# A transformer layer on one core: longer warm-up, angle tables written later, and one column block of the last layer norm on TensorE and ScalarE

## The chip, the cores and the metric

The kernel runs on one core of one Trainium2 chip. The metric is the device time of one execution in microseconds; the kernel before has a median of 1452.82 us over three runs.

## The reference, cut to what matters

One decoder layer for 256 tokens of width 2048, in float32. The projection feeds a retention branch and a sliding-window attention branch; their gated sum goes through an output projection, a layer norm, a SwiGLU feed-forward block and a second layer norm.

```python
proj = h @ w_in
ret = retention_branch(rq, rk, rv, rg, ...)              # rotary angles from positions
att = sliding_window_sink_attention(aq, ak, av, sinks, positions)
merged = sigmoid(gate_a) * ret + sigmoid(gate_b) * att
h = layer_norm(ALPHA * h + merged @ w_out, ln1_g, ln1_b)
ffn = (silu(h @ w_gate) * (h @ w_up)) @ w_down
h = layer_norm(ALPHA * h + ffn, ln2_g, ln2_b)            # (z - mean) * rsqrt(var + eps) * g + b
```

## The kernel before, in words

Every large product is a stream of *chunks*. A chunk gives 512 output columns for both halves of the tokens (t = 0 and t = 1, 128 tokens each). Its weights come in blocks by the queue of SyncE (`raw`), ScalarE rounds them (`wh`, line 192), VectorE makes the rest (`wl`, line 193), and TensorE adds three matmuls for each 128 rows of the weight and each t: `wh` by `xh` (line 208), `wl` by `xh` (209), `wh` by `xl` (210). So line 209 can't begin before the whole `wl` of its block is there. The first chunk is special: its weights come together with the columns of x in nine blocks (`xraw`), and x itself is split into `xh` and `xl` (lines 422 and 423) on the way. It is followed by four chunks of attention queries, four for retention's queries and keys, and the rest.

Beside the stream, small jobs (Python generators) are stepped twice after each step of the stream by `pump`; what they write is interleaved with the stream. The tile framework then schedules: it sets each engine's final order by its own model of what is ready, so the order in which the code is written is not the order in which an engine gets its instructions. Names in the code and in the rows:

- `tables` (from line 428): sine and cosine of the rotary angles; some 35 VectorE instructions on 128x272 values, then three sines on ScalarE.
- `akv_bg` (504): rotates the attention keys and transposes them to `kT`; `attention` (524): one job for each key head g and each t. It makes its scores (line 543) in two banks of the pool `mx`. The eight query heads of a group lie in pairs over the upper and lower 64 partitions (u = 0, 1); a score matmul uses 64 rows of TensorE, those of u = 0 write one bank, those of u = 1 the other. VectorE reads them from the bank (line 546).
- `NWARM` matmuls on zeros (403) run before the first data is there.
- `ln2` (740): for the last layer norm, mean and variance, then for each of four column blocks two VectorE instructions (lines 728 and 729) and a DMA of the result.

Of the kernel before, what the change touches and what calls it, by code (L numbers as in the profile page):

```python
# [9 lines left out]
F32 = mybir.dt.float32  # L10
F32R = mybir.dt.float32r
I32 = mybir.dt.int32
AF = mybir.ActivationFunctionType
ALU = mybir.AluOpType
RIGHT = "right"

P = 128
SEQ = 256
DM = 2048
DFF = 5632  # L20
C = 512
# [3 lines left out]
HD = 64  # L25
NSPL = 3
NSPL0 = 3
NWARM = 2
AKD = 7
NQ = 3  # L30
NGEN = 3
PC = 2
# [23 lines left out]
NFR = 136  # L56
LINE = 32
NFL = 144
# [37 lines left out]
def layer_kernel(ctx, tc, a, out):  # L96
    nc = tc.nc
# [12 lines left out]
    def bank(kind, shape):  # L110
        if "all" in psp:
            return psp["all"].tile(shape, F32, name="bank")
        return psp[kind].tile(shape, F32, name=kind)
# [25 lines left out]
    def drain():  # L139
        while bg:  # L140
            pump(1)
# [215 lines left out]
    jobs = {}  # L357
# [3 lines left out]
    ident = cst[:, 0:P]  # L361
# [4 lines left out]
    def bcast_cols(dram, c0, n):  # L366
        return dram[0:1, c0:c0 + n].broadcast_to([P, n])
# [33 lines left out]
    for i in range(NWARM):  # L401
        wp = bank("tr", [P, C])
        nc.tensor.matmul(wp, lhsT=warm[:, 0:P], rhs=warm[:, P:P + C], start=True, stop=True)

    XS = [1, 1, 2, 2, 2, 2, 2, 2, 2]
    xraw = {}

    def x_dma(b):
        k = sum(XS[:b])
        r = ini.tile([P, max(XS), SEQ + C], F32, name="xraw", bufs=XB)  # L410
        nc.sync.dma_start(out=r[:, 0:XS[b]], in_=a["xw"][:, k:k + XS[b]])
        xraw[b] = r
        if b == 2:
            nc.scalar.dma_start(out=cst[:, 0:NC0], in_=a["consts"][:, 0:NC0])
            xraw["pos"] = ini.tile([P, LINE], I32, name="posi")[:, 0:2]
            nc.scalar.dma_start(out=xraw["pos"], in_=a["pos"])

    def x_cast(b):
# [7 lines left out]
        return xh[:, k, t * P:(t + 1) * P], xl[:, k, t * P:(t + 1) * P]  # L426

    def tables():
        posi = xraw["pos"]
        posf = ini.tile([P, 2], F32, name="posf")  # L430
        nc.vector.tensor_copy(out=posf, in_=posi)
        ang = ini.tile([P, 2, NFR], F32, name="ang")
        for t in range(2):
            nc.vector.tensor_scalar(out=ang[:, t], in0=freq, scalar1=posf[:, t:t + 1], scalar2=None, op0=ALU.mult)
        yield
        SH = [P, 2, NFR]
        cur = ang
        digs = []
        for i, e in enumerate((20, 8, -4)):
            m = 1.5 * 2.0 ** (23 + e)  # L440
            d = ini.tile(SH, F32, name=f"dig{i}")
            nc.vector.tensor_scalar(out=d, in0=cur, scalar1=m, scalar2=m, op0=ALU.add, op1=ALU.subtract)
            nc.vector.tensor_sub(out=cur, in0=cur, in1=d)
            digs.append(d)
            yield
        c20 = _digits(20, -12, -24)
        c8 = _digits(8, -12, -24)
        c4 = _digits(-4, -18, -30)
        M0 = 1.5 * 2.0 ** 23
        hi = None  # L450
        tmp = ini.tile(SH, F32, name="ttmp")
        for i, cc in enumerate((c20, c8, c4)):
            t = ini.tile(SH, F32, name=f"th{i}")
            nc.vector.tensor_scalar(out=t, in0=digs[i], scalar1=cc[0], scalar2=None, op0=ALU.mult)
            nc.vector.tensor_scalar(out=tmp, in0=t, scalar1=M0, scalar2=M0, op0=ALU.add, op1=ALU.subtract)
            nc.vector.tensor_sub(out=t, in0=t, in1=tmp)
            if hi is None:
                hi = t
            else:
                nc.vector.tensor_add(out=hi, in0=hi, in1=t)  # L460
            yield
        nc.vector.tensor_scalar(out=tmp, in0=hi, scalar1=M0, scalar2=M0, op0=ALU.add, op1=ALU.subtract)
        nc.vector.tensor_sub(out=hi, in0=hi, in1=tmp)
        nc.vector.tensor_scalar(out=cur, in0=cur, scalar1=INV2PI, scalar2=None, op0=ALU.mult)
        for d, k in ((digs[1], c8[2]), (digs[0], c20[2]), (digs[2], c4[2]), (digs[2], c4[1]), (digs[1], c8[1]), (digs[0], c20[1])):
            nc.vector.scalar_tensor_tensor(out=cur, in0=d, scalar=k, in1=cur, op0=ALU.mult, op1=ALU.add)
            yield
        nc.vector.tensor_add(out=hi, in0=hi, in1=cur)
        yield
        nc.vector.tensor_scalar(out=tmp, in0=hi, scalar1=M0, scalar2=M0, op0=ALU.add, op1=ALU.subtract)  # L470
        nc.vector.tensor_sub(out=hi, in0=hi, in1=tmp)
        nc.vector.tensor_scalar(out=hi, in0=hi, scalar1=TWO_PI, scalar2=PI_LO, op0=ALU.mult, op1=ALU.min)
        nc.vector.tensor_scalar(out=hi, in0=hi, scalar1=-PI_LO, scalar2=None, op0=ALU.max)
        nc.vector.scalar_tensor_tensor(out=tmp, in0=hi, scalar=-1.0, in1=hi, op0=ALU.mult, op1=ALU.max)
        nc.scalar.activation(out=sinr, in_=hi, func=AF.Sin)
        nc.scalar.activation(out=sinn, in_=hi, func=AF.Sin, scale=-1.0)
        nc.scalar.activation(out=cosr, in_=tmp, func=AF.Sin, scale=-1.0, bias=halfpi)
        yield

    def rot_small(x16, t, n):  # L480

        sh = [P, n, 2, 8]
        t1 = ap_.tile([P, n, 2, 8], F32, name="ra")
        t2 = ap_.tile([P, n, 2, 8], F32, name="rb")
        cs = cosr[:, t, 128:136].unsqueeze(1).unsqueeze(1).broadcast_to(sh)
        sp = sinr[:, t, 128:136].unsqueeze(1).broadcast_to([P, n, 8])
        sn = sinn[:, t, 128:136].unsqueeze(1).broadcast_to([P, n, 8])
        nc.vector.tensor_mul(out=t1, in0=x16, in1=cs)
        nc.vector.tensor_mul(out=t2[:, :, 0], in0=x16[:, :, 1], in1=sn)
        nc.vector.tensor_mul(out=t2[:, :, 1], in0=x16[:, :, 0], in1=sp)  # L490
        nc.vector.tensor_add(out=x16, in0=t1, in1=t2)
# [7 lines left out]
    def done_akv(ch, t):  # L499
        nc.scalar.copy(out=kvt[:, t], in_=ch.acc[t])  # L500
        if t:
            jobs["akv"] = Job(akv_bg())

    def akv_bg():
        for _ in range(AKD):
            yield
        for t in range(2):
            rot_small(kvt[:, t, 0:256].rearrange("p (h d) -> p h d", d=HD)[:, :, 0:16].rearrange("p h (a b) -> p h a b", a=2), t, NKV)
            kd = ap_.tile([P, NKV, 2, HD], F32, name="kd")
            kv_ = kvt[:, t, 0:256].rearrange("p (h d) -> p h d", d=HD)  # L510
            for u in range(2):
                nc.vector.tensor_copy(out=kd[:, :, u], in_=kv_)
            yield
            ps = transpose4([kd[:, g].rearrange("p a d -> p (a d)") for g in range(NKV)])
            yield
            nc.scalar.copy(out=kT[:, :, t * P:(t + 1) * P], in_=ps)
            yield
# [4 lines left out]
        Job(attention(g, t, q), [jobs["akv"]])  # L522

    def attention(g, t, q):
        rot_small(q.rearrange("p (h d) -> p h d", d=HD)[:, :, 0:16].rearrange("p h (a b) -> p h a b", a=2), t, 8)
        yield
        ps = transpose4([q[:, i * P:(i + 1) * P] for i in range(4)])
# [191 lines left out]
    def norm(t):  # L719
        mv = small.tile([P, 2], F32, name="mv")  # L720
        rs = small.tile([P, 1], F32, name="rsd")
        nc.vector.bn_aggr(out=mv, in_=sc["stats"][:, t])
        rsqrt(rs, mv[:, 1:2])
        return mv, rs
# [6 lines left out]
    def ln1(t):  # L731
# [3 lines left out]
        for c in range(4):  # L735
            ln(t, gains["ln1_g"], gains["ln1_b"], slice(c * C, (c + 1) * C), mv, rs)
            ps = transpose4([hres[:, t, (c * 4 + i) * P:(c * 4 + i + 1) * P] for i in range(4)])
            split_evict(hh[:, c * 4:c * 4 + 4, tk], hl[:, c * 4:c * 4 + 4, tk], ps)

    def ln2(t):  # L740
        mv, rs = norm(t)
        for c in range(4):
            cols = slice(c * C, (c + 1) * C)
            ln(t, gains["ln2_g"], gains["ln2_b"], cols, mv, rs)
            (nc.scalar if c % 2 else nc.sync).dma_start(out=out[t * P:(t + 1) * P, cols], in_=sc["hres"][:, t, cols])

    def preload_sqrt():
        t = small.tile([P, 1], F32, name="rs")
# [2 lines left out]
    def resid(ch, t, c, scale, stats):  # L751
        hres = sc["hres"]
        cols = slice(c * C, (c + 1) * C)
        nc.vector.scalar_tensor_tensor(out=hres[:, t, cols], in0=hres[:, t, cols], scalar=scale, in1=ch.acc[t], op0=ALU.mult, op1=ALU.add)
        if stats:
            nc.vector.bn_stats(out=sc["stats"][:, t, c], in_=hres[:, t, cols])
# [40 lines left out]
    def done_d(ch, t, half, c):  # L797
        if half == 2 and c == 2 and t == 1:
            preload_sqrt()
        resid(ch, t, c, 1.0 if half else ALPHA, half == 2)  # L800
        if half == 2 and c == 3:
            ln2(t)

# [86 lines left out]
        i += -(-n // KS)  # L890
    jobs["tab"] = Job(tables())
    stream.run(mark_0, PC)
    drain()
    tc.keep_in_program_order(nc.sync.dma_start(out=msk, in_=a["consts"][:, NC0:]))
    tc.keep_in_program_order(nc.sync.dma_start(out=sinks, in_=a["sinks"]))
    isc.close()
# [51 lines left out]
    for nm, tg in (("ln2_g", "hh"), ("ln2_b", "hl")):  # L948
        gains[nm] = hp.tile([P, DM], F32, name=tg)
        nc.sync.dma_start(out=gains[nm], in_=bcast_cols(a[nm], 0, DM))  # L950
    stream.run(len(stream.steps), PC)
    drain()

# [75 lines left out]
```

## Time and profile before

| | |
|---|---|
| median of 3 runs | 1452.82 us (1452.8 to 1454.17) |
| the profiled execution | 1452.66 us, its span 1450.9 us |
| TensorE busy | 1434.0 us (99%) |
| VectorE busy | 961.8 us (66%) |
| ScalarE busy | 654.1 us (45%) |
| HBM | 189 GB/s over the span |

The span is what the profiler saw from the first to the last instruction; the 1.76 us between it and the time lie around it. Busy shares are averages over the whole run. PE is TensorE, PEld its weight load, DVE VectorE, ACT ScalarE, SP SyncE.

### The profile page before, as it was taken

Reading aid. Unit: us, or ns where it says so; the run is one execution under the profiler, and the core shown is the slowest. Engines: PE = TensorE matmul, PEld = TensorE weight load, DVE = VectorE, ACT = ScalarE, POOL = GpSimd, SP = SyncE. Lnnn points to the kernel's source line nnn. Section 1 sums busy time; section 2 is a strip of 40 time slices with the busy share of each in tenths; the row PEclk is TensorE's granted clock in tenths of the full one; section 3 lists DMA queues with packets and bytes.
Section 4 is the critical chain, followed back from the end, with each engine's and each line's share of the span. In section 5 each row is a group of like instructions: output and inputs, shape, how many; then the busy total and the mean of one; then the engine's idle time right before and its main releaser. Section 6 shows DMA issues by size and latency. Waiting matters only on the chain.

```text
span 1450.9 us, 15948 instructions
## 1 busy us (share of the span) xinstructions
PE 1434.0 (99%) x6562; PEld 1177.6 (81%) x6562; DVE 961.8 (66%) x1011; ACT 654.1 (45%) x617; POOL 0.9 (0%) x6
## 2 busy tenths in 40 slices
PE   9999999999999999999999999999999999999997
PEld 6888888878788787888877888888888888888885
DVE  8565555455555555555698987457998755798756
ACT  6464644343443434433344544334455433454431
POOL 0000000000000000000000000000000000000000
PEclk9999999999999999999999999999999999999998
DMA  8643334555555455576455555555655555655561
GB/s 298 240 148 127 117 117 145 186 186 194 185 206 180 172 199 179 196 282 214 145 204 203 181 214 185 180 197 203 217 189 192 191 198 191 215 192 211 195 228 74
DMA packets 40232, 274.73 MB, mean 189 GB/s; under 512 B 4704, under 2 KB 4832, under 8 KB 8160
## 3 DMA queue, kind: packets, MB, share of 16 engines
q1 hardware_dynamic: 39296, 272.53, 53.5%
q10 hardware_dynamic: 864, 1.19, 0.2%
q8 instruction: 51, 0.84, 0.2%
q14 instruction: 21, 0.17, 0.0%
HBM read 271.60 MB, written 2.10 MB: 189 GB/s over the span
## 4 chain that ended last, share of the span: by engine, by line
PE 96%; DVE 3%; DMA 0%; issue 0%; ACT 0%; DVEq 0%; ACTq 0%
PE acc L208 15%; PE acc L210 15%; PE acc L209 15%; PE bank L298 10%; PE bank L300 9%; PE bank L299 9%; PE bank L210 6%; PE bank L208 6%; PE bank L209 5%; PE tr L496 2%; PE mx L572 1%; PE mx L543 1%; DVE wl L193 1%; PE bank L496 1%; PE mx L636 0%; DVE hres L728 0%
## 5 line engine op out<-in xcount | busy, mean ns | idle before, releaser
L193 DVE TENSOR_TENSOR wl<-raw,wh 128x2048 fp32r<-128x2048 f32 x164 | 375.7, 2291 | 305.6 <-ACT wh L192 305.2
L192 ACT CAST wh<-raw 128x2048 fp32r<-128x2048 f32 x164 | 313.3, 1910 | 437.7 <-PE acc L210 243.8
L208 PE MATMUL acc<-wh,xh 128*128 128x512 f32 x800 | 317.6, 398 | 1.3 <-ACT wh L192 1.3
L209 PE MATMUL acc<-wl,xh 128*128 128x512 f32 x800 | 314.4, 393 | 0.8 <-DVE wl L193 0.8
L210 PE MATMUL acc<-wh,xl 128*128 128x512 f32 x800 | 313.2, 391 | 0.0
L278 ACT CAST wh<-raw 128x1536 fp32r<-128x1536 f32 (+1 forms) x80 | 140.2, 1752 | 126.9 <-PE bank L300 77.8
L279 DVE TENSOR_TENSOR wl<-raw,wh 128x1536 fp32r<-128x1536 f32 (+1 forms) x80 | 166.4, 2088 | 25.3 <-ACT wh L278 24.9
L298 PE MATMUL bank<-wh,hh 128*128 128x512 f32 x460 | 179.7, 391 | 0.0
L208 PEld LDWEIGHTS acc<-wh,xh 128*128 128x128 f32 x800 | 150.7, 188 | 35.8 <-ACT wh L192 2.9
L300 PE MATMUL bank<-wh,hl 128*128 128x512 f32 x460 | 179.1, 389 | 0.0
L299 PE MATMUL bank<-wl,hh 128*128 128x512 f32 x460 | 179.0, 389 | 0.0
L209 PEld LDWEIGHTS acc<-wl,xh 128*128 128x128 f32 x800 | 150.6, 188 | 33.7 <-issue 2.2
L210 PEld LDWEIGHTS acc<-wh,xl 128*128 128x128 f32 x800 | 150.5, 188 | 33.0 <-issue 1.3
L208 PE MATMUL bank<-wh,ph 128*128 128x512 f32 x352 | 137.2, 390 | 0.0
L210 PE MATMUL bank<-wh,pl 128*128 128x512 f32 x352 | 137.0, 389 | 0.0
L209 PE MATMUL bank<-wl,ph 128*128 128x512 f32 x352 | 136.9, 389 | 0.0
L300 PEld LDWEIGHTS bank<-wh,hl 128*128 128x128 f32 x460 | 86.3, 188 | 18.0
L299 PEld LDWEIGHTS bank<-wl,hh 128*128 128x128 f32 x460 | 86.4, 188 | 17.8
L298 PEld LDWEIGHTS bank<-wh,hh 128*128 128x128 f32 x460 | 86.4, 188 | 17.6
L278 ACT CAST th<-tsum 128x2048 fp32r<-128x2048 f32 x30 | 57.5, 1915 | 52.1 <-DVE tsum L266 35.1
L279 DVE TENSOR_TENSOR tl<-tsum,th 128x2048 fp32r<-128x2048 f32 x30 | 68.8, 2292 | 13.9 <-ACT th L278 13.6
L210 PEld LDWEIGHTS bank<-wh,pl 128*128 128x128 f32 x352 | 66.1, 188 | 13.7
(187 smaller groups left out, 1483.5 us busy)
## 6 DMA issues: line engine op xcount, KB each, us to landing
raw<-in_w_in SPq DMA_DIRECT2D x96, 1024.0 KB, 4.9
raw<-in_w_gu SPq DMA_DIRECT2D x88, 1024.0 KB, 4.9
raw<-in_w_down SPq DMA_DIRECT2D x44, 1024.0 KB, 4.8
raw<-in_w_out SPq DMA_DIRECT2D x16, 1024.0 KB, 4.9
xraw<-in_xw SPq DMA_DIRECT2D x7, 768.0 KB, 6.0
hres<-in_x SPq DMA_DIRECT2D x1, 2048.0 KB, 7.6
gg<-in_gn_g SPq DMA_DIRECT2D x4, 256.0 KB, 3.5
gb<-in_gn_b SPq DMA_DIRECT2D x4, 256.0 KB, 3.6
```

Of the source, the lines that this page charges most:

```text
L192: nc.scalar.copy(out=h[:, 0:m], in_=r)
L193: nc.vector.tensor_sub(out=l[:, 0:m], in0=r, in1=h[:, 0:m].bitcast(F32))
L208: nc.tensor.matmul(self.acc[t], lhsT=xh, rhs=wh[:, j], start=st, stop=False)
L209: nc.tensor.matmul(self.acc[t], lhsT=xh, rhs=wl[:, j], start=False, stop=False)
L210: nc.tensor.matmul(self.acc[t], lhsT=xl, rhs=wh[:, j], start=False, stop=sp)
L278: nc.scalar.copy(out=h_, in_=r)
L279: nc.vector.tensor_sub(out=l_, in0=r, in1=h_.bitcast(F32))
L298: nc.tensor.matmul(self.acc[p], lhsT=xh, rhs=wh[:, j], start=st, stop=False)
L299: nc.tensor.matmul(self.acc[p], lhsT=xh, rhs=wl[:, j], start=False, stop=False)
L300: nc.tensor.matmul(self.acc[p], lhsT=xl, rhs=wh[:, j], start=False, stop=sp)
L496: nc.tensor.transpose(ps[:, i], s, ident)
L543: nc.tensor.matmul(sps[u][:, i], lhsT=qT[u * HD:(u + 1) * HD, h // 2], rhs=kT[u * HD:(u + 1) * HD, g, 0:W], start=True, stop=True)
```

## The change

There are four edits. The warm-up gets a third matmul and one of half width. The job `tables` lets 14 pumps pass before it begins, keeps its values in the `att` tile, which is not yet used then, issues its six multiply-adds in one step, and is no longer drained behind the first chunk; the key job now depends on it in place of waiting seven pumps. An attention job of t = 1 lets three pumps pass first. In `ln2`, block 1 of t = 1 is computed as three matmuls into a bank, with diagonal matrices made by ScalarE, and copied out by ScalarE; a product of it, `zg`, is made earlier on VectorE. Also the result's DMAs are shared out anew between the queues.

```diff
-NWARM = 2
-AKD = 7
+NWARM = 3
+TD = 14
...
+    wp = bank("tr", [P, C])
+    nc.tensor.matmul(wp[:, 0:SEQ], lhsT=warm[:, 0:P], rhs=warm[:, P:P + SEQ], start=True, stop=True)
...
     def tables():
+        for _ in range(TD):
+            yield
+        room = att.rearrange("p t d -> p (t d)")
...
         for d, k in ((digs[1], c8[2]), (digs[0], c20[2]), (digs[2], c4[2]), (digs[2], c4[1]), (digs[1], c8[1]), (digs[0], c20[1])):
             nc.vector.scalar_tensor_tensor(out=cur, in0=d, scalar=k, in1=cur, op0=ALU.mult, op1=ALU.add)
-            yield
+        yield
...
         if t:
-            jobs["akv"] = Job(akv_bg())
+            jobs["akv"] = Job(akv_bg(), [jobs["tab"]])
     def akv_bg():
-        for _ in range(AKD):
-            yield
...
     def attention(g, t, q):
+        for _ in range(3 * t):
+            yield
...
+    CP = 1
+
     def ln2(t):
         mv, rs = norm(t)
+        if t:
+            cols = slice(CP * C, (CP + 1) * C)
+            g, b, zg, ps = gains["ln2_g"], gains["ln2_b"], sc["zg"], bank("acc", [P, C])
+            nm = small.tile([P, 1], F32, name="rsn")
+            nc.vector.tensor_scalar(out=nm, in0=mv[:, 0:1], scalar1=-1.0, scalar2=None, op0=ALU.mult)
+            dg = sc["dg"]
+            nc.scalar.activation(out=dg[:, 0], in_=ident, func=AF.Copy, scale=rs)
+            nc.scalar.activation(out=dg[:, 1], in_=dg[:, 0], func=AF.Copy, scale=nm)
+            nc.tensor.matmul(ps, lhsT=ident, rhs=b[:, cols], start=True, stop=False)
+            nc.tensor.matmul(ps, lhsT=dg[:, 0], rhs=zg, start=False, stop=False)
+            nc.tensor.matmul(ps, lhsT=dg[:, 1], rhs=g[:, cols], start=False, stop=True)
+            nc.scalar.copy(out=sc["hres"][:, t, cols], in_=ps)
+            nc.scalar.dma_start(out=out[t * P:(t + 1) * P, cols], in_=sc["hres"][:, t, cols])
         for c in range(4):
+            if t and c == CP:
+                continue
             cols = slice(c * C, (c + 1) * C)
             ln(t, gains["ln2_g"], gains["ln2_b"], cols, mv, rs)
-            (nc.scalar if c % 2 else nc.sync).dma_start(out=out[t * P:(t + 1) * P, cols], in_=sc["hres"][:, t, cols])
+            (nc.scalar if c == 3 and not t else nc.sync).dma_start(out=out[t * P:(t + 1) * P, cols], in_=sc["hres"][:, t, cols])
...
+        if half == 2 and c == CP and t == 1:
+            nc.vector.tensor_mul(out=sc["zg"], in0=sc["hres"][:, t, c * C:(c + 1) * C], in1=gains["ln2_g"][:, c * C:(c + 1) * C])
...
     stream.run(mark_0, PC)
-    drain()
```

What stands on the engines after the scheduler shows where the edits end up. First VectorE, from the `wl` of the second block of x on to that of the third; before (`ang`, `dig`, `th`, `ttmp` are values of the tables):

```order
L193 TENSOR_TENSOR wl_127<-xraw,wh_126 128x512
L442 TENSOR_SCALAR dig_153<-ang 128x272
L443 TENSOR_TENSOR ang<-ang,dig_153 128x272
L454 TENSOR_SCALAR th_197<-dig_153 128x272
L442 TENSOR_SCALAR dig_170<-ang 128x272
L455 TENSOR_SCALAR ttmp<-th_197 128x272
L443 TENSOR_TENSOR ang<-ang,dig_170 128x272
L423 TENSOR_TENSOR xl<-xraw,xh 128x512
L442 TENSOR_SCALAR dig_173<-ang 128x272
L193 TENSOR_TENSOR wl_135<-xraw,wh_134 128x1024
```

And now, the same place (all values of the tables are parts of `att`):

```order
L193 TENSOR_TENSOR wl_131<-xraw,wh_130 128x512
L453 TENSOR_SCALAR att<-att 128x2x136
L454 TENSOR_TENSOR att<-att 128x2x136
L465 TENSOR_SCALAR att<-att 128x2x136
L453 TENSOR_SCALAR att<-att 128x2x136
L466 TENSOR_SCALAR att<-att 128x2x136
L454 TENSOR_TENSOR att<-att 128x2x136
L425 TENSOR_TENSOR xl<-xraw,xh 128x512
L453 TENSOR_SCALAR att<-att 128x2x136
L193 TENSOR_TENSOR wl_139<-xraw,wh_138 128x1024
```

The same instructions of the tables stand at the same place, although the code now writes them 14 pumps later; only the last ones, the six multiply-adds among them, move behind the last block of x.

Then TensorE in the attention of the third key head, t = 1 (`mx` with its number is the bank, `kT` and `qT` the transposed keys and queries). One of its two score groups before:

```order
L496 MATMUL tr_1284<-cst_80,sm_1154 128x128 x4
L543 MATMUL mx_1292<-kT_95,qT_1247 128x256
L543 MATMUL mx_1293<-kT_95,qT_1247 128x256
L543 MATMUL mx_1292<-kT_95,qT_1247 128x256
L543 MATMUL mx_1293<-kT_95,qT_1247 128x256
L496 MATMUL tr_1302<-cst_80,sm_1084 128x128 x4
```

And the first score group of the attention of the same kind that stands there now, with the beginning of its second:

```order
L583 MATMUL mx_980<-kvt_96,pT_1173 128x64 x4
L554 MATMUL mx_1222<-kT_95,qT_1175 128x256 x2
L507 MATMUL tr_1229<-cst_80,sm_1095 128x128 x4
L208 MATMUL acc_1189<-wh_1108,xh_91 128x512
L209 MATMUL acc_1189<-wl_1109,xh_91 128x512
L210 MATMUL acc_1189<-wh_1108,xl_92 128x512
L208 MATMUL acc_1193<-wh_1108,xh_91 128x512
L554 MATMUL mx_1223<-kT_95,qT_1175 128x256 x2
L209 MATMUL acc_1193<-wl_1109,xh_91 128x512
L554 MATMUL mx_1239<-kT_95,qT_1175 128x256 x2
```

Four matmuls that took turns between two banks have become two pairs, each on one bank, with matmuls of the stream between them.

Last, the end of the program for t = 1, on ScalarE behind the last rounding of weights; this is what stands there now (before: the two rows of line 377, and DMAs):

```order
L377 ACTIVATE rsd<-rs 128x1
L761 ACTIVATE sl<-cst,rsd 128x128
L762 ACTIVATE sl<-sl,rsn 128x128
L766 COPY hres<-bank 128x512
L767 DMA out_h<-hres 128x512
```

And on TensorE, behind the last matmul of the stream:

```order
L210 MATMUL bank<-wh,pl 128x512
L763 MATMUL bank<-hl,cst 128x512
L764 MATMUL bank<-sh,sl 128x512
L765 MATMUL bank<-hh,sl 128x512
```

`sl` holds the two diagonal matrices and `sh` the product `zg`; TensorE now has work after the stream's end, and VectorE has two instructions of 128x512 fewer there.

## Rows read from the trace of the kernel before

**Rows 1.** The page: the span, and the shares of the chain that ended last

```profile
span 1450.9 us, 15948 instructions
...
PE 96%; DVE 3%; DMA 0%; issue 0%; ACT 0%; DVEq 0%; ACTq 0%
```

**Rows 2.** Waits of PE, whole run: total us, times, the longest

```profile
PE acc L209 <- DVE wl L193: 1.2, 2, 0.8
```

**Rows 3.** Timeline of the start: start us, us, instruction, idle before it

```profile
1.45 3.78 PE L403 MATMUL tr<-warm 128*128 128x512 f32 x4 [1.45 <-POOL warm L399]
...
6.56 1.22 PE L208 MATMUL acc<-wh,xh 128*128 128x512 f32 x2 [1.32 <-ACT wh L192]
...
7.58 0.63 PE L209 MATMUL acc<-wl,xh 128*128 128x512 f32 x1
...
8.01 0.63 PE L210 MATMUL acc<-wh,xl 128*128 128x512 f32 x1
...
10.23 0.68 DVE L423 TENSOR_TENSOR xl<-xraw,xh 128x512 fp32r<-128x512 f32 x1
...
11.04 1.22 DVE L193 TENSOR_TENSOR wl<-xraw,wh 128x1024 fp32r<-128x1024 f32 x1
...
12.31 0.50 PE L209 MATMUL acc<-wl,xh 128*128 128x512 f32 x1 [0.75 <-DVE wl L193]
```

**Rows 4.** Timeline where the first chunk ends

```profile
24.16 0.43 DVE L466 SCALAR_TENSOR_TENSOR ang<-dig,ang 128x272 f32<-128x272 f32 x1
...
28.92 2.29 DVE L193 TENSOR_TENSOR wl<-raw,wh 128x2048 fp32r<-128x2048 f32 x1
...
31.53 0.39 PE L208 MATMUL acc<-wh,xh 128*128 128x512 f32 x1
```

**Rows 5.** Timeline of PE: score matmuls (two records for each in float32)

```profile
77.01 1.16 PE L543 MATMUL mx<-kT,qT 64*128 64x128 f32 x16
...
127.22 1.98 PE L543 MATMUL mx<-kT,qT 64*128 64x256 f32 x8
...
150.50 1.13 PE L543 MATMUL mx<-kT,qT 64*128 64x256 f32 x8
...
160.56 1.13 PE L543 MATMUL mx<-kT,qT 64*128 64x256 f32 x4
...
186.57 1.16 PE L543 MATMUL mx<-kT,qT 64*128 64x128 f32 x8
...
204.87 1.53 PE L543 MATMUL mx<-kT,qT 64*128 64x256 f32 x8
```

**Rows 6.** Windows, line 543 alone: stretch, length, busy and (records)

```profile
31.46:264.60 233.14, 19.30 (x128) 13.70 (x128) 1.00 0.43 150
```

**Rows 7.** Timeline of the end

```profile
1440.24 0.69 DVE L754 SCALAR_TENSOR_TENSOR hres<-hres,bank 128x512 f32<-128x512 f32 x1 [0.90 <-PE bank L210]
...
1442.91 0.20 ACT L377 ACTIVATE rsd<-rs 128x1 f32<-128x1 f32 x1 [7.95 <-DVE rs L376]
...
1444.77 1.41 DVE L728 SCALAR_TENSOR_TENSOR hres<-hres,mv,hh 128x512 f32<-128x512 f32 x2
...
1446.10 1.41 DVE L729 SCALAR_TENSOR_TENSOR hres<-hres,rsd,hl 128x512 f32<-128x512 f32 x2
```

**Rows 8.** Windows of the end: PE, PEld, DVE, ACT, POOL, then PEclk, granted clock

```profile
1442.00:1443.40 1.40, 0.00 (x0) 0.00 (x0) 1.40 (x4) 0.20 (x1) 0.00 (x0) 1.00 0.00 0
1443.60:1450.90 7.30, 0.00 (x0) 0.00 (x0) 3.90 (x6) 0.00 (x0) 0.00 (x0) 0.50 0.38 144
```

**Rows 9.** Timeline, other stretches: a copy, an activation, float32 matmuls

```profile
31.03 1.28 ACT L500 COPY kvt<-acc 128x512 f32<-128x512 f32 x2 [0.39 <-PE acc L210]
...
83.54 0.38 ACT L555 ACTIVATE sm<-sm,nm 128x128 f32<-128x128 f32 x1
...
306.54 1.02 PE L636 MATMUL mx<-v,st_all 128*128 128x512 f32 x2
...
307.40 1.02 PE L638 MATMUL mx<-v,st_all 128*128 128x512 f32 x2
```

More of the change, by code (lines that the diff above doesn't have):

```diff
@@ L414, in x_dma @@
             nc.scalar.dma_start(out=cst[:, 0:NC0], in_=a["consts"][:, 0:NC0])
-            xraw["pos"] = ini.tile([P, LINE], I32, name="posi")[:, 0:2]
+            xraw["pos"] = xp.tile([P, LINE], I32, name="posi")[:, 0:2]
             nc.scalar.dma_start(out=xraw["pos"], in_=a["pos"])
@@ L428, in tables, with take @@
     def tables():
+        for _ in range(TD):
+            yield
+        room = att.rearrange("p t d -> p (t d)")
+        at = [0]
+        def take():
+            v = room[:, at[0]:at[0] + 2 * NFL].rearrange("p (t d) -> p t d", t=2)[:, :, 0:NFR]
+            at[0] += 2 * NFL
+            return v
         posi = xraw["pos"]
-        posf = ini.tile([P, 2], F32, name="posf")
+        posf = xp.tile([P, LINE], F32, name="posf")[:, 0:2]
         nc.vector.tensor_copy(out=posf, in_=posi)
-        ang = ini.tile([P, 2, NFR], F32, name="ang")
+        ang = take()
         for t in range(2):
@@ L435, in tables @@
         yield
-        SH = [P, 2, NFR]
         cur = ang
@@ L440, in tables @@
             m = 1.5 * 2.0 ** (23 + e)
-            d = ini.tile(SH, F32, name=f"dig{i}")
+            d = take()
             nc.vector.tensor_scalar(out=d, in0=cur, scalar1=m, scalar2=m, op0=ALU.add, op1=ALU.subtract)
@@ L450, in tables @@
         hi = None
-        tmp = ini.tile(SH, F32, name="ttmp")
+        tmp = take()
         for i, cc in enumerate((c20, c8, c4)):
-            t = ini.tile(SH, F32, name=f"th{i}")
+            t = take()
             nc.vector.tensor_scalar(out=t, in0=digs[i], scalar1=cc[0], scalar2=None, op0=ALU.mult)
@@ L950, in layer_kernel @@
         nc.sync.dma_start(out=gains[nm], in_=bcast_cols(a[nm], 0, DM))
+    sc["zg"] = hp.tile([P, C], F32, name="sh")
+    sc["dg"] = hp.tile([P, 2, P], F32, name="sl")
     stream.run(len(stream.steps), PC)
```

## Prediction

> **What bounds the kernel now.** I read the page first: the chain that ended last is TensorE for 96% of a span of 1450.9 us [rows 1]. So an edit is worth something only if it takes time from TensorE's stream, adds to it, or moves the stretch after its last matmul. Next I asked who TensorE waits for. The table of waits is short: the one that VectorE causes in the stream, line 209 on `wl`, is 1.2 us in two times, the longest 0.8 [rows 2]. The timeline of the start shows where that longest one is: line 209 of the third block begins at 12.31, just behind the `wl` that VectorE began at 11.04 [rows 3]. From there to the end of the first chunk TensorE runs without a stop. The timeline of the end shows the other place: after the stream VectorE works alone from 1440.24 to 1447.51 (1446.10 + 1.41) [rows 7], and the span ends 3.4 us after that, with the last transfer. Between these two, everything on TensorE counts one for one, the attention's small matmuls too.
>
> **Warm-up and tables.** Two warm matmuls are four records and take 3.78 us from 1.45 on [rows 3], so about 0.85 us a record and a tail. Three and a half of them end near 1.45 + 7 x 0.85 = 7.4 us, behind the 6.56 at which the first real matmul began. What hides this is the wait: TensorE has 14 matmuls to do before it meets line 209 at 12.31. Before, it had done them by 11.56 (12.31 less the 0.75 of idle time in that row), 5.0 us after the first [rows 3]. They began at a spacing of 0.43 us (7.58 to 8.01: 512 columns at the lower level, 1.2 GHz), which over all 14 would be 6.0 us, so the clock rose on the way. If the 14 take as long again, they end at 12.4, 0.1 us late; if the clock never rose, at 13.4, 1.1 late; if the unbroken warm-up (the 1.32 us pause at 6.56 is gone) lets it rise earlier, TensorE only waits longer. I take 0, with 0 and +1.1 as bounds.
>
> Would that wait go, since the tables come later? The order says no: VectorE has the same six table instructions ahead of `xl`, and one between `xl` and `wl`, in the same place as before. The code is written later, but the scheduler pulls it forward again. So `xl` begins at 10.23 and `wl` at 11.04 as they did [rows 3], and the prize, at most the 0.8 us wait, is not won. At the end of the chunk the six multiply-adds, 0.43 us each [rows 4], stand in a row in front of the first large `wl`. Five of them and some more have left the blocks of x, which then end about a microsecond and a half earlier, so that the 2.29 us cast begins near the 28.92 of before, some 0.3 us later at most. It would end by 31.5; TensorE reaches the chunk at 31.53 and needs `wl` two matmuls after that [rows 4]. Nothing is lost there. I take 0 for both edits; bounds -0.8 and +0.3.
>
> **The order in the attention.** This is the side effect that I price highest. Rows show what score matmuls cost by how they stand. Eight records of 64x256 that take turns between the two banks last 1.13 us; four records that stand alone on one bank last 1.13 us as well [rows 5]. With 64x128 it is 16 records for 1.16 and 8 records for 1.16 [rows 5]. So a group that is split by banks costs twice: two matmuls on different halves of the 128 rows run at one time, two on the same half don't. Two pairs back to back lie between, 1.98 and 1.53 [rows 5].
>
> All 128 records sum to 19.30 us before [rows 6]. Now I count the new order by class. Taking turns: two groups of 64x128 (2 x 1.16 = 2.32) and two half-groups of 64x256 (2 x 1.13 = 2.26). By bank: four halves of 64x128 (4 x 1.16 = 4.64), eight lone pairs of 64x256 (8 x 1.13 = 9.04), one double pair (1.98) and two more pairs among transposes (2.26). The sum is 22.50, that is 3.2 us more. I take +3.0, since the last two pairs stand among other float32 work that fills the array. The rest of the attention has the same instructions. Lower bound: if each of the ten pairs costs half of the cheaper double pair, 0.77 in place of 1.13, it is 3.6 us less, -0.6. Upper bound: at one place TensorE also waits for a bank that VectorE reads only behind a weight cast of 2.29 us [rows 4], +5.3.
>
> **The tail.** VectorE loses two instructions of 128x512: four of them take from 1444.77 to 1447.51 [rows 7], 2.74 us, so two are 1.35. It gains a tiny one (the negated mean), about 0.1. Its last result comes at 1446.25 and the span would end 1.25 us earlier. In competition stands the new path: `rsd` ends at 1443.2 (1442.91 + 0.20, and 0.1 for the tiny one) [rows 7]; the first diagonal by the nearest row 0.38 [rows 9], 1443.6; the second is ready before its matmul. A float32 matmul of 128x512 begins 0.86 us after another at the full clock (306.54 to 307.40) [rows 9], so two end at 1445.3 and a tail of 0.16; the copy is 0.64 (1.28 for two) [rows 9], 1446.1. The DMA issues as late as VectorE's last. Both end together, so -1.2. At the lower level each of the two takes 1.7 (3.78 for two in the warm-up [rows 3], less the tail): 1443.6 + 3.4 + 0.3 + 0.64 = 1447.95, 0.44 behind the result of before, so the tail is +0.5. The granted clock was 1.00 up to 1443.40 and 0.50 from 1443.60 on [rows 8], 3.2 us after the last matmul; now line 763 keeps TensorE busy to about 1441.1, and only 2.5 us pass to the next one. I take the full clock. `zg` is one VectorE instruction of about 0.7 us in a stretch in which VectorE waits for ScalarE; it is free. On SyncE's queue the masks and the sinks stand between the same weight blocks as before; two of the result's blocks change their queue, which with both queues idle then is nothing.
>
> **Sum.** Against the profiled execution: 1452.66 + 0 + 3.0 - 1.2 = 1454.46. The median of the runs is 0.16 above that execution, so 1454.6. A difference under 0.2% (2.9 us) is about what can't be told from no change here.
>
> **Rivals.**
> 1. *Split scores are cheap.* For it: the double pair at 204.87 takes 1.53, less than two lone pairs [rows 5]. Against it: lone pairs cost the full 1.13. Then the attention gives about 0 and the time is 1452.82 - 1.2 = 1451.6.
> 2. *Banks run late (slower).* By the order VectorE reads half of a score group, then does a 2.29 us cast [rows 4], then reads the other half, at two places. If TensorE comes to the next pair on that bank before the read is over, it stands still for up to the cast: 1454.6 + 2.3 = 1456.9, and more if it happens twice. It decides where the work between takes less than cast and reads; I count 10 and 15 matmuls of the stream and one pair between, at least 10 x 0.22 + 1.13 = 3.3 us, so it is close at the first place only.
> 3. *The clock falls before the late matmuls.* The tail gives +0.5 in place of -1.2, so 1456.3. The row of the granted clock speaks for a fall after 3.2 us, the gap is shorter, and part of it is filled. The Trainium skill (TensorE: Matmul & The Clock Gate, Part 1) says that the throttled state is the default and activity has to release it; by that rule the two matmuls could run at 1.2 GHz, which is this rival. The trace agrees so far that the clock did fall in this stretch.
> 4. *The start is won after all.* If the scheduler's order did not matter because the table instructions find other gaps, the 0.8 wait goes [rows 2], and with cheap splits the time is 1450.8; to pass 0.2% it would also need a shorter attention than before.
>
> **How the numbers follow.** Forecast 0.50 (1453.2 to 1455.7), rival 1 0.20, rival 2 0.14, rival 3 0.10, rival 4 0.06. Rivals 2 and 3 and a little of the forecast's upper edge are slower by over 0.2%: 0.25. Rival 4 and the far end of rival 1 give 0.07 for faster; the rest, 0.68, is within 0.2%. The range reaches from rival 1 less a little, 1451.2, to rival 2, 1457.0.
>
> **What would show it.** The wait of line 209 near 12.3 us should stand as before, after a first real matmul near 7 us. Line 554 should be busy for about 22.5 us where line 543 was for 19.30. VectorE's last instruction should end about 6.0 us after the last addition begins (7.3 before), with the ScalarE copy near the same time. The prediction is wrong if the wait at 12.3 has gone, if line 554's sum stays near 19, or if TensorE shows waits for VectorE between 60 and 250 us.

## The result and the profile after

The changed kernel takes 1479.49 us (median of 6 runs, 1478.22 to 1479.65) against 1452.8 us before: a ratio of 1.0181, 95% interval 1.0170 to 1.0192. It is 26.7 us slower; the prediction was 1454.6 us with a range up to 1457.0. The prediction was wrong.

The page of the profiled execution after: span, busy time, and the shares of the chain that ended last.

```profile
span 1477.4 us, 15970 instructions
...
PE 1465.5 (99%) x6572; PEld 1182.2 (80%) x6572; DVE 964.3 (65%) x1011; ACT 656.3 (44%) x620; POOL 0.9 (0%) x6
...
PE 81%; DVE 2%; ACT 0%; issue 0%; ACTq 0%
```

TensorE has ten records more than before and is busy for 31.5 us more (1434.0 before). So the time did not go into a wait: TensorE's work itself became longer. Its table of waits after, whole run (total us, times, the longest), says the same; it answers to [rows 2].

```profile
PE bank L764 <- ACT sl L761: 2.6, 1, 2.6
PE acc L209 <- DVE wl L193: 1.8, 3, 1.3
```

The first is the new work at the end. The second grew by 0.6 us in all, because the first matmuls came sooner (6.30 in place of 6.56), soon followed each other by 0.23 to 0.24 us (0.43 before, at the lower clock), and met the same `wl`. Both are small beside 26.7.

Where did the busy time go? Three stretches in which TensorE runs nothing but the stream show it: one of the input product (`xh`, `xl`), one of the output projection (`mh`, `ml`), one of gate and up (`hh`, `hl`, and sums of them). Windows of TensorE before, from the start of the first such matmul to that of the last: stretch, length, busy and records, granted clock, share of the DMA engines, GB/s.

```profile
308.49:364.52 56.03, 56.03 (x248) 1.00 0.57 196
638.84:720.78 81.94, 81.94 (x364) 1.00 0.63 230
778.68:848.64 69.96, 69.96 (x308) 1.00 0.57 201
```

And the same matmuls after:

```profile
315.62:373.25 57.63, 57.63 (x248) 1.00 0.56 193
654.30:736.23 81.93, 81.93 (x364) 1.00 0.63 230
794.91:866.60 71.69, 71.69 (x308) 1.00 0.56 198
```

The first stretch holds 247 intervals: 56.03 / 247 = 0.2268 us a matmul before, 0.2333 after. In the third it is 0.2271 and 0.2328 (308 intervals). In the second nothing changed. The granted clock is 1.00 in all six, so the clock is not the cause. The starts also give the time lost up to there: 7.1 us by 315.62, 15.5 at 654.30, still 15.5 at 736.23, where the output projection ends. No operand of the slow stretches was edited, yet they are slower everywhere, and only there. The groups of TensorE by line sort by the operand too (records, busy us, mean ns of one). Before:

```profile
L208 PE MATMUL acc<-wh,xh 128*128 128x512 f32 x800 | 317.6, 398 | 1.3 <-ACT wh L192 1.3
...
L298 PE MATMUL bank<-wh,hh 128*128 128x512 f32 x460 | 179.7, 391 | 0.0
...
L208 PE MATMUL bank<-wh,ph 128*128 128x512 f32 x352 | 137.2, 390 | 0.0
```

And after:

```profile
L208 PE MATMUL acc<-wh,xh 128*128 128x512 f32 x800 | 320.7, 401 | 0.2 <-ACT wh L192 0.2
...
L298 PE MATMUL bank<-wh,hh 128*128 128x512 f32 x460 | 182.1, 396 | 0.0
...
L208 PE MATMUL bank<-wh,ph 128*128 128x512 f32 x352 | 137.2, 390 | 0.0
```

What distinguishes them is where the operands lie. The edit of `ln2` takes a new tile, `rsn`, from the pool `small`; the pool has four buffers of each tile, 32 bytes a partition each, so it grew by 128 bytes, and everything placed behind it moved up. The placement in the built programs (start in a partition, in bytes, and that modulo 256):

```
operand                    before         after          experiment 1
wh, wl  (stream)           42368 (128)    42368 (128)    42368 (128)
xh, xl  (input product)   103296 (128)   103424 (  0)   103296 (128)
hh, hl  (gate and up)     113024 (128)   113152 (  0)   113024 (128)
mh, ml  (output proj.)    196480 (128)   196480 (128)   196480 (128)
ph, pl  (down product)    196480 (128)   196480 (128)   196480 (128)
wh1,wl1 (first chunk)     194048 (  0)   194304 (  0)   194176 (128)
```

For each pair the place of `wh`, `xh`, `hh`, `mh`, `ph` or `wh1` is given; its low part, the other buffers and the slices of 512 or 2048 bytes lie at the same place modulo 256. Slow are the products whose two operands differ there. It even explains the first chunk, which went the other way: `xh` against `wh1` was 128 bytes apart before and is not now, and its matmuls are spaced 0.233 us before and 0.227 after.

The start answers to [rows 3, 4] (timeline after):

```profile
6.30 0.51 PE L208 MATMUL acc<-wh,xh 128*128 128x512 f32 x1
...
12.19 0.50 PE L209 MATMUL acc<-wl,xh 128*128 128x512 f32 x1 [1.29 <-DVE wl L193]
...
28.94 2.29 DVE L193 TENSOR_TENSOR wl<-raw,wh 128x2048 fp32r<-128x2048 f32 x1
```

The wait at 12.2 stands where it stood, and the first large cast starts at 28.94 where it started at 28.92. TensorE begins the second chunk at 30.93 in place of 31.53: the first chunk's matmuls are those that became faster. The score matmuls answer to [rows 6]:

```profile
31.00:290.00 259.00, 22.75 (x128) 15.50 (x128) 1.00 0.43 150
```

22.75 us, 22.5 forecast. The end answers to [rows 7, 8], first as a timeline, then as windows:

```profile
1469.51 0.40 ACT L761 ACTIVATE sl<-cst,rsd 128x128 f32<-128x128 f32 x1
...
1469.96 2.07 PE L764 MATMUL bank<-sh,sl 128*128 128x512 f32 x2 [2.60 <-ACT sl L761]
...
1471.83 1.58 PE L765 MATMUL bank<-hh,sl 128*128 128x512 f32 x2
1471.91 0.75 DVE L740 SCALAR_TENSOR_TENSOR hres<-hres,rsd,hl 128x512 f32<-128x512 f32 x1
1473.45 0.59 ACT L766 COPY hres<-bank 128x512 f32<-128x512 f32 x1 [3.10 <-PE bank L765]
```

```profile
1467.40:1469.90 2.50, 0.00 (x0) 0.00 (x0) 2.43 (x8) 0.59 (x2) 0.00 (x0) 0.93 0.02 7
1469.90:1471.90 2.00, 1.94 (x3) 0.91 (x4) 1.98 (x3) 0.41 (x2) 0.00 (x0) 0.50 0.25 96
```

In this execution the clock fell in the 2.6 us pause (granted 0.50 from 1469.90 on), and the copy by ScalarE ends 1.4 us behind VectorE (1474.04 and 1472.66).

### The profile page after: what moved, and what is told of

Its sections match the earlier page's. It is cut to its first block, busy times and chain, and to the rows that moved or that the text cites. A ratio compares the mean times of both kernels' runs of the same rounds, so it can differ in the third digit from the quotient of the medians.

```text
span 1477.4 us, 15970 instructions
## 1 busy us (share of the span) xinstructions
PE 1465.5 (99%) x6572; PEld 1182.2 (80%) x6572; DVE 964.3 (65%) x1011; ACT 656.3 (44%) x620; POOL 0.9 (0%) x6
## 4 chain that ended last, share of the span: by engine, by line
PE 81%; DVE 2%; ACT 0%; issue 0%; ACTq 0%
PE acc L210 11%; PE acc L209 11%; PE acc L208 11%; PE bank L298 10%; PE bank L299 10%; PE bank L300 10%; PE bank L208 5%; PE bank L209 5%; PE bank L210 5%; PE tr L507 1%; PE bank L507 1%; PE mx L647 0%; DVE wl L193 0%; DVE hres L739 0%; PE mx L621 0%; PE mx L649 0%
## 5 line engine op out<-in xcount | busy, mean ns | idle before, releaser
L209 PE MATMUL acc<-wl,xh 128*128 128x512 f32 x800 | 318.0, 398 | 1.5 <-DVE wl L193 1.5
L210 PE MATMUL acc<-wh,xl 128*128 128x512 f32 x800 | 316.6, 396 | 0.0
```

What stands on the lines that cost most here:

```text
L209: nc.tensor.matmul(self.acc[t], lhsT=xh, rhs=wl[:, j], start=False, stop=False)
L210: nc.tensor.matmul(self.acc[t], lhsT=xl, rhs=wh[:, j], start=False, stop=sp)
```

## The experiments

**Theory A, addresses:** the stream's pace hangs on where its weight operand and its moving operand start relative to each other, modulo 256 bytes. (The weight operand is the one that TensorE loads and holds, `lhsT` in the code: here `xh`, `hh` and the like. The moving operand is `rhs`: here the rounded weights of the layer, `wh` and `wl`.) **Theory B, order:** the warm-up or the attention's order brought TensorE into a slower pace that lasts. Experiments 1 to 4 tell these apart, 5 to 8 test the terms of the prediction, 9 turns the measured table into a forecast, 10 and 11 test the clock at the end and a version that keeps what is good.

**1. The changed kernel without its new tile.**

```diff
-            nm = small.tile([P, 1], F32, name="rsn")
+            nm = small.tile([P, 8], F32, name="nm")[:, 0:1]
```

> The changed kernel with one edit: the negated mean goes into a tile that exists already (nm) in place of the new tile rsn. So the pool small is not 128 bytes larger, and xh, xl, hh, hl, sh, sl, kT and all else behind it lie where they lay before. Nothing else differs. Theory A (addresses): a matmul of the stream is spaced 0.227 us when its weight operand and its moving operand start at the same place modulo 256 bytes, 0.233 us when they are 128 bytes apart modulo 256; the new tile moved xh, xl, hh and hl by 128 bytes and left wh and wl. A expects a spacing of 0.227 all along the run, the first chunk too, and 1479.5 - 26 = 1453.5 us (1452 to 1455). Theory B (order): the longer warm-up or the new order in the attention brought TensorE into a slower pace that lasts. B expects 0.233 as after, and 1478 to 1480 us.

Measured: 1455.66 us (11 runs), ratio to before 1.0021, interval 1.0012 to 1.0029. The first of the three stretches, and the score matmuls:

```profile
312.07:368.10 56.03, 56.03 (x248) 1.00 0.57 198
...
31.00:290.00 259.00, 22.86 (x128) 15.58 (x128) 1.00 0.43 150
```

56.03 us again, and 0.227 us in the first chunk too. By the medians 23.8 of the 26.7 us go with the 128 bytes. The last matmul of the stream shows how much of that is the stream's; it begins like this before, after and in this experiment:

```profile
1439.82 0.39 PE L210 MATMUL bank<-wh,pl 128*128 128x512 f32 x1
...
1466.12 0.39 PE L210 MATMUL bank<-wh,pl 128*128 128x512 f32 x1
...
1443.42 0.39 PE L210 MATMUL bank<-wh,pl 128*128 128x512 f32 x1
```

The stream has its matmuls in the same order here and in the changed kernel, and is 22.7 us shorter. The other 1.0 us of the two profiled executions lies behind it (11.3 us to the end of the span in the changed kernel, 10.3 here), where the clock fell in the one and held in the other; that the tile has a part in this isn't shown. The expectation of 1453.5 us (1452 to 1455) charged all 26 us to the addresses and was missed; 2.8 us stay for the edits. Theory B is out.

**2 and 3. The kernel before, moved by 128 and by 256 bytes.** No instruction is added (for 3: 64 in place of 32).

```diff
+    padp = ctx.enter_context(tc.tile_pool(name="padp", bufs=1))
+    padp.tile([P, 32], F32, name="padt")
     small = ctx.enter_context(tc.tile_pool(name="small", bufs=4))
```

> The kernel before with one edit: an unused tile of 128 bytes ahead of the pool small. No instruction is added. Theory A (addresses modulo 256): xh, hh and their low parts are 128 bytes off wh and wl, so the matmuls of the 24 chunks behind the first and of the feed-forward gate and up products are spaced 0.233 us, those of the output projection (mh, ml) and of the down product (ph, pl) stay at 0.227, and the time is about 1452.8 + 26 = 1479 us (1476 to 1481). Theory B (order) expects no difference: 1452.8 us within 1.5.

> The kernel before with an unused tile of 256 bytes ahead of the pool small. Theory A expects the time of before, 1452.8 us within 1.5, and a spacing of 0.227 where it was. A rival to A, theory C (any shift, as by distance to the end of the memory or to other tiles), expects at least the 26 us of a shift by 128, so 1479 us or more.

Measured: 1476.05 us with 128 bytes (four runs, 1474.4 to 1477.2; ratio 1.0163, 1.0147 to 1.0178), 1452.9 with 256 (1.0001, 0.9992 to 1.001). The first stretch (247 intervals in both) with 128 bytes,

```profile
312.27:369.67 57.40, 57.40 (x249) 1.00 0.56 192
```

and with 256:

```profile
308.63:364.66 56.03, 56.03 (x248) 1.00 0.57 195
```

An unused tile alone makes the kernel before 23.2 us slower; twice the tile costs nothing. So it is the place modulo 256 bytes that matters, not the shift as such: theory C is out.

**4. The cost by itself.** Matmuls alone; beside them VectorE only copies one result after each group. Each group is a line like this, with its own offsets in bytes for the weight operand and the moving operand:

```diff
+    for x, y, f, l in go(48, st, mv, 32, 0): nc.tensor.matmul(p, lhsT=x, rhs=y, start=f, stop=l)
```

> Leaves out the whole layer and writes zeros; it measures the disputed cost alone. 22 groups of matmuls of 128x128 by 128x512, each group on a source line of its own: 16 to start with, then 48 with the weight operand 0, 32, 64, 96, 128, 160, 192 and 224 bytes on and the moving operand 0 on, the same eight with the moving operand 128 on, four with weight and moving operand at (0, 64), (64, 64), (128, 192), (192, 192), and two groups of 16 in float32. Theory A expects about 0.227 us a matmul where both start at the same place modulo 256, and 0.233 at a distance of 128; what the distances between do is open. Theory D (the weight operand's own place alone decides) expects the same eight values for both places of the moving operand. If nothing beside TensorE is needed for the effect it shows here; if all groups read the same, it needs the other engines' traffic.

Timeline of TensorE: the start of each group of 48, so the difference of two starts is the time of 48 matmuls.

```profile
11.08 11.05 PE L122 MATMUL p<-mv,st 128*128 128x512 f32 x48
21.97 11.35 PE L125 MATMUL p<-mv,st 128*128 128x512 f32 x48
33.16 11.36 PE L128 MATMUL p<-mv,st 128*128 128x512 f32 x48
44.36 11.40 PE L131 MATMUL p<-mv,st 128*128 128x512 f32 x48
55.60 11.32 PE L134 MATMUL p<-mv,st 128*128 128x512 f32 x48
66.76 11.37 PE L137 MATMUL p<-mv,st 128*128 128x512 f32 x48
77.96 11.16 PE L140 MATMUL p<-mv,st 128*128 128x512 f32 x48
88.95 11.36 PE L143 MATMUL p<-mv,st 128*128 128x512 f32 x48
100.15 11.35 PE L146 MATMUL p<-mv,st 128*128 128x512 f32 x48
...
144.74 11.05 PE L158 MATMUL p<-mv,st 128*128 128x512 f32 x48
155.63 11.35 PE L161 MATMUL p<-mv,st 128*128 128x512 f32 x48
```

Lines 122 to 143 have the weight operand 0, 32, ... 224 bytes on and the moving operand at 0: 10.89 us at distance 0 (0.2269 us a matmul), 11.16 to 11.24 at 32 to 160, 10.99 at 192 (0.2290), 11.20 at 224 (0.2333). Lines 146 and 158 have the moving operand at 128: with the weight operand at 0 it is now 11.19, at 128 it is 10.89. So the distance decides, and theory D is out. Over all 20 groups the four at distance 0 take 10.89 to 10.90 us, the four at 192 take 10.99 to 11.01, the twelve others 11.16 to 11.24. So it doesn't need the other engines' work of the layer. Two float32 groups, at distance 0 and 128, last 13.89 and 13.90 us: no effect there. What in the chip makes it, these runs don't show.

**5. The attention's order taken back as well** (on top of experiment 1).

```diff
-TD = 14
+TD = 12
...
     def attention(g, t, q):
-        for _ in range(3 * t):
-            yield
```

> The changed kernel without the new tile rsn (as the first experiment) and without the three pumps of delay in the attention of t = 1; the tables let 12 pumps pass in place of 14. In this order the score matmuls stand in the same groups as in the kernel before. Theory E (split scores): the 2.8 us by which the first experiment is behind the kernel before are the score matmuls' order (line 554 is busy for 22.86 us there, line 543 for 19.30 before), and the rest of the edits give about 1 us back. Expects a score line at 19.3 us busy and 1455.66 - 3.6 - 0.5 = 1451.5 us (1450.8 to 1452.3). Rival F: head or tail cost the 2.8 us; then the score line falls to 19.3 and the time stays at 1454.5 or more.

Measured: 1452.43 us (ratio 0.9994, 0.9985 to 1.0003), 3.2 us less than experiment 1. The score matmuls:

```profile
31.00:290.00 259.00, 19.30 (x128) 13.70 (x128) 1.00 0.45 156
```

19.30, as before the change; 3.56 us less busy, 3.2 us less time by the medians. Theory E holds. The medians understate it, since the end's clock divides the runs of both kernels into groups (experiment 10), seven of eleven in the faster group in experiment 1 and five of eleven here. In the two profiled executions the clock held at the end, and the stream's last matmul begins 3.7 us earlier here (1439.75 and 1443.42), though chunk two begins 0.4 us later (31.41 and 31.00). So the order costs 4.1 us: the score line's 3.56, and the transposes of `rt` (line 507), 5.4 us busy in experiment 1 and 4.8 here. The median is 0.9 us above the 1451.5 expected and just beyond that range; experiment 10 finds the cause at the end.

**6. The attention's delay alone, on the kernel before.**

```diff
     def attention(g, t, q):
+        for _ in range(3 * t):
+            yield
```

> The kernel before with one edit: an attention job of t = 1 lets three pumps pass. By its order ten groups become eight lone pairs, four lone fours, two double pairs, and two groups of each shape that take turns: 4 x 1.16 + 8 x 1.13 + 2 x 1.98 + 2 x 1.16 + 2 x 1.13 = 22.2 us by the rows of before. Theory E expects the score line at 22.2 and 1452.9 + 3 = 1455.9 us (1455 to 1457). Rival F expects 1452.9 within 0.7.

Measured: 1454.82 us, ratio 1.0015 (1.0006 to 1.0023). The score line is 22.10 us busy (22.2 counted from the rows of before), 2.8 more, and the time 2.0 more, below the 1455 to 1457 expected. The trace shows why: from the start of chunk two to the end of the attention TensorE loses 2.6 us, and then gains 0.6 where the kernel before (and experiment 5) waits 0.5 us at line 298 for `pl`; that wait is missing in this one's table. Rival F is out.

**7. The end alone, on the kernel before**, with the mean in an existing tile: the `ln2` edit, `zg`, `dg` and the queues of the result as in the change.

```diff
+            nm = small.tile([P, 8], F32, name="nm")[:, 0:1]
```

> The kernel before with the edit of the last layer norm alone, its negated mean in a tile that exists already, so that nothing moves. Two outcomes by the traces so far: where the clock holds, the two late matmuls begin 0.96 us apart as in the first experiment and the end comes 0.8 to 1.2 us earlier, 1451.7 to 1452.1; where it falls, as in the profile of the changed kernel (the first took 2.07 us), the end comes 0.2 to 0.5 later, 1453.1 to 1453.4. A mix gives a median between, with runs in both groups.

Measured: 1452.96 us, ratio 1.0001 (0.9992 to 1.0009). The eleven runs fall into three groups: two runs at 1451.85 and 1451.96, six at 1452.74 to 1453.08, three at 1453.99 to 1454.48. The first group is the outcome expected with the clock held; the second lies just below the 1453.1 to 1453.4 expected without it. The third comes from the start, as far as its one profiled execution (1453.99) shows: there the clock fell behind the wait of line 209, and TensorE began chunk two 1.5 us later than before (33.02 and 31.53). So in the median the edit of the end gives nothing. That the clock falls before its matmuls more often than not is read from these groups; in this one profile it fell during the late matmuls (the first took 1.29 us, the second 1.92).

**8. Tables that can't be ready earlier.** On top of experiment 5 the positions are loaded behind the last block of x.

```diff
         xraw[b] = r
+        if b == len(XS) - 1:
+            nc.sync.dma_start(out=xraw["pos"], in_=a["pos"])
...
-            nc.scalar.dma_start(out=xraw["pos"], in_=a["pos"])
```

> The fifth experiment, and the positions are loaded behind the last block of x on SyncE's queue, so that no instruction of the tables can be ready before. In its order VectorE has xl and wl of the first chunk without a table instruction between. Theory G: the wait of line 209 at the third block (1.3 us) is the tables' doing; it goes, chunk two begins about 1.2 us earlier, and the time is 1451.5 - 1.2 = 1450.3 us. Rival H: ten table instructions (0.3 to 0.44 us each, some 3.6 us) now stand ahead of the first weight cast of 2.29 us, and TensorE waits for that at the beginning of the second chunk by 1 to 2 us: 1451.3 to 1452.3.

Measured: 1450.84 us (1450.3 expected), ratio 0.9986 (0.9977 to 0.9995), 1.6 us less than experiment 5. Its wait of line 209:

```profile
PE acc L209 <- DVE wl L193: 1.0, 2, 0.5
```

The longest is 0.5, still at the third block, where it was 1.3; the other comes much later, in the first chunk of gate and up. Rival H's wait at the second chunk isn't there. Theory G holds in its sign; 0.5 of the 1.3 us is left, and is no longer the tables'. Nor is all of the 1.6 us: experiments 10 and 11, in which the clock is held at the end, differ by the tables alone, and by 0.8 us. That is what the wait lost; the rest is that the median of experiment 5 lies in the slower group of the end.

**9. A forecast from the table of experiment 4.** As experiment 2, with 48 in place of 32 (192 bytes).

> The kernel before with an unused tile of 192 bytes ahead of the pool small, so that xh and hh start 192 bytes (or, modulo 256, -64) from wh and wl. In the fourth experiment the groups at that distance began 10.99 us after each other for 48 matmuls, those at the same place 10.89 us, those at all other distances 11.16 to 11.25 us. If the stream follows that table, it is spaced 0.229 us in the 24 chunks of the input product and in gate and up, and the time is 1452.8 + 26 x 0.10 / 0.31 = 1461 us (1459 to 1464). If any distance but zero costs the same in the kernel, it is 1476 as with 128 bytes.

Measured: 1460.93 us, ratio 1.0054 (1.004 to 1.0067); 1461 was forecast. The forecast scaled an estimate of 26 us for a distance of 128 bytes; scaled from the 23.2 of experiment 2 it is 1460.3, so the last 0.6 us of the hit are luck. The first stretch (249 records, 247 intervals):

```profile
310.34:366.87 56.53, 56.53 (x249) 1.00 0.56 195
```

0.2289 us a matmul, 0.2290 in the group by itself. The table holds in the kernel at this distance.

**10. The clock held at the end** (on top of experiment 5).

```diff
             nc.tensor.matmul(ps, lhsT=ident, rhs=b[:, cols], start=True, stop=False)
+            for i in range(2):
+                hold = bank("acc", [P, C])
+                nc.tensor.matmul(hold, lhsT=ident, rhs=zg, start=True, stop=True)
```

> The fifth experiment with two more float32 matmuls of 128x512 between line 763's matmul and the two that wait for the diagonals; their result is not used. They fill some 1.7 us of the 2.6 us in which TensorE waited. Theory: the runs of the fifth experiment split into 1451.6 to 1452.1 and 1452.4 to 1452.8 by whether the clock held for the two late matmuls; now it holds each time, all runs lie at 1451.5 to 1452.1, and the median falls from 1452.43 to 1451.7. If the two groups have another cause, both stay.

Measured: 1451.54 us, ratio 0.999 (0.9982 to 0.9999). All eleven runs lie at 1451.43 to 1451.84; the upper group of experiment 5 (six of eleven, 1452.43 to 1452.75) is gone. The late matmuls:

```profile
1443.31 1.12 PE L765 MATMUL bank<-sh,sl 128*128 128x512 f32 x2 [0.88 <-ACT sl L759]
...
1444.27 1.02 PE L766 MATMUL bank<-hh,sl 128*128 128x512 f32 x2
```

They begin 0.96 us apart, against 1.87 in the changed kernel's profile. So work that nobody needs, in a pause of 2.6 us, made the median 0.9 us faster. Experiment 5's fastest run (1451.56) is as fast without it, and its profile, a run of the faster group, has the 0.96 too: the two matmuls take the slower group away, they don't make a faster end.

**11. Both together** (experiments 8 and 10).

> The eighth experiment (tables behind the first chunk by their data, score order as before, nothing moved) with the same two filling matmuls. Expects 1450.7 us, with no run above 1451.0, against 1450.84 (1450.66 to 1451.43) without them; and faster than the kernel before by 2.1 us (0.14%).

Measured: 1450.78 us (1450.63 to 1451.0), ratio 0.9984 (0.9975 to 0.9993): 2.0 us faster than before and 28.7 faster than the change. This has the later load of the positions and the two filling matmuls in it; the change's own edits, once nothing moves and the scores keep their order, are worth the 0.4 us of experiment 5, which its interval can't tell from nothing.

## Why the prediction was wrong

**The step that failed** is in "What bounds the kernel now" and "The tail". The prediction says that everything on TensorE counts one for one, and then counts only matmuls that the change adds or reorders; the stream's own 5862 were taken to cost what they did. Of the new tile it says that VectorE "gains a tiny one (the negated mean), about 0.1". The instruction did cost 0.14 us. Its tile cost 23.8 us by the medians (experiment 1), 22.7 of them in the stream, by moving `xh`, `xl`, `hh` and `hl` (and the sums `sh`, `sl`) 128 bytes against the operands that they are multiplied with. That is 4326 matmuls (5862 less 96 of the first chunk, 384 of the output projection and 3 x 352 of the down product) at 0.0053 us more each on average: 0.0065 and 0.0057 in the two slow stretches, about 0.004 where the attention's jobs stand between. No row of before shows an address, but the placement could have been compared; the order, which was compared, doesn't show it. None of the four rivals held it.

**The warm-up and the tables: right, with one thing missed.** The wait of line 209 stayed (1.29 us), the first large cast came at 28.94, as said. The reason was right as well: it was the order of VectorE. When data held the tables back, 0.8 us were won (experiment 11 against 10). The first real matmul came at 6.30, not near 7, since the added warm-up matmuls were faster than the first ones (six records take 4.70 us, four took 3.78). The missed gain is the placement again: by the table above the first chunk's operands now lie at the same place modulo 256, and it ends about 0.5 us earlier (experiment 1: chunk two at 31.00, against 31.53).

**The attention: the mechanism right, the size somewhat low.** +3.0 us was taken. 3.2 was measured by the medians of experiments 1 and 5 (which also differ by two pumps of the tables) and 4.1 by their traces, with a line at 22.75 to 22.86 us where 22.5 was counted; the transposes, which the prediction took as unchanged, are the other 0.6. Alone on the kernel before it is +2.0 (experiment 6). Rival 1 is out. Rival 2, TensorE standing for a late bank, doesn't appear in the table of waits.

**The tail: the mechanism right, the choice between its two values wrong.** It was -1.2 at the full clock, +0.5 at the lower one, and the full clock was taken. Both happen, each smaller than forecast. From the last matmul of the stream to the end of the span it is 11.1 us before, 10.3 with the clock held (experiments 1, 5 and 10), 11.3 in the changed kernel's profile: -0.8 and +0.2. VectorE's last result does come about 6.1 us after the last addition begins (7.3 before; about 6.0 were forecast), but 3.7 to 3.8 us pass behind it where 3.4 did; why, is open. That head and end together give -1.2 (experiment 10 against 1452.77), the size forecast for the end alone, is luck: 0.4 of it is the earlier end of the first chunk. Alone the end gives nothing in the median (experiment 7). Rival 3 is what the changed kernel's profile shows and, by the groups of times, most executions of it and of experiments 5 and 7; in experiment 1 seven of eleven lie in the faster group. The rule of the Trainium skill that stood beside it (TensorE: Matmul & The Clock Gate, Part 1: throttled is the default, and activity releases it) agrees with these rows: granted 0.50 behind the pause, and no fall where two matmuls filled it. In the profiles of experiments 1 and 5 the same pause of 2.6 us brought no fall.

**The sum:** by the traces, the stream's last matmul comes 26.3 us later than before: 22.7 for the addresses, 4.1 for the attention, -0.5 for the first chunk. With the +0.2 behind it this is the 26.5 us between the two spans. By medians it is 23.8, 3.2 and -0.4 (1452.43 against 1452.84), where the first two terms carry the end's clock. Without the addresses it is 1455.66, 1.1 above the forecast and within its range.

## What to carry to other kernels

A new tile is an edit to every tile behind it: compare the placement of the big operands before and after, and give a small value a place in a tile that exists. Where all matmuls of a stage get slower by the same 2 to 3% at a full clock, while another stage with the same shapes does not, look at where their operands lie before looking at their order. And a matmul that ends the program after a pause can run at the lower clock (here it did in some executions and not in others); price it so, unless something keeps TensorE busy in the pause.

## What the runs showed of the hardware

- The spacing of matmuls of 128x128 by 128x512 in fp32r (the type of the rounded operands `wh`, `xh` and the like) depends on the distance of the two operands' starts modulo 256 bytes: 0.227 us at 0, 0.229 at 192, 0.232 to 0.234 at the other multiples of 32. The distance is the start of the weight operand (`lhsT`) less that of the moving one (`rhs`). Distances 0, 128 and 192 were seen in the full kernel as well, the others only in experiment 4. It isn't symmetric: 64 costs 11.20 us for 48, 192 costs 10.99. Float32 shows nothing of it at 128.
- In some executions the clock falls behind the wait of 1.3 us at the start. In experiment 6's profiled execution (1456.21 us, one of two out of eleven runs that lie 1.4 us above the others) it did, though TensorE had run at 0.24 us a matmul just before that wait. Windows of TensorE there, with the granted clock behind the records:

```profile
12.30:13.00 0.70, 0.64 (x2) 0.69 0.92 386
13.00:15.00 2.00, 2.00 (x6) 0.50 0.95 292
15.00:16.00 1.00, 1.00 (x4) 0.51 1.13 375
16.00:17.00 1.00, 1.00 (x5) 1.00 0.74 203
```

It came back by 16 us. Experiment 7's profile shows the same. That the wait alone does it isn't shown: in the changed kernel and in experiments 1, 5 and 10 the wait is as long and the clock stayed at 1.00, and in experiment 3's profile (1452.84 us) it fell at 7.7 us, before that wait. The kernel before has five runs of 33 in the same comparison that lie as far above the others (1454.13 to 1454.33, the others 1452.5 to 1453.03); none of them was profiled, so the cause there is open.
